# Longer weight runs, a reordered load queue and a new split of the casts in a batched matmul

## The chip, the cores and the metric

The kernel runs on one core of a Trainium2 chip. The metric is the device time of one execution in microseconds, the median of several runs. A profiled execution gives a trace; its span, from the first to the last instruction, is 1 to 2 us shorter than the timed figure. TensorE appears as PE (its weight loads as PEld), VectorE as DVE, ScalarE as ACT, GpSimd as POOL and SyncE, which issues all transfers, as SP.

## The reference

```python
b1, b2, m, k, n = 8, 16, 256, 512, 384
x:      (8, 16, 256, 512) float32
weight: (8, 16, 512, 384) float32
out = np.matmul(x, weight)          # 128 independent products
```

The inputs are 167.77 MB and the output 50.33 MB, so 218.1 MB have to cross between memory and the core.

## The kernel before

The 128 products are worked in 32 groups of G = 4. For each group the kernel loads weights and x as float32, casts both to bf16, transposes x on TensorE, copies the transposes out of PSUM, multiplies, copies the products out of PSUM and stores them.

```python
XS, WS, OS = 2, 2 * G // D, 4          # buffers: x, weight halves (D = 2), output
def load(e, t, U, s):                   # SyncE, group n
    for d in range(G // D):             # two transfers, 12 KB per partition each
        e.wait_ge(w_cast, ...)          # the slot's casts are done
        e.dma_start(w_sb[slot][:], w_rows[...].rearrange("(p k) n -> p k n", k=S * KO))
    e.wait_ge(x_cast, ...)
    e.dma_start(x_sb[s % XS][:], ...)   # 16 KB per partition

def prepare(e, t, U, s):                # VectorE
    ...                                 # 8 casts of 64 partitions x 1536 columns
    for q in range(T):                  # T = 4: transposes out of PSUM
        e.wait_ge(t_made, ...)
        e.tensor_copy(out=x_t[...], in_=pt[...].bitcast(bf16))

# ScalarE: 4 casts of x, then 4 copies of products out of PSUM
# SyncE, in its loop: load(n + 4); store(n)
```

TensorE does 16 transposes and 128 matmuls a group. A store of group n is issued after the loads of group n + 4; the copy of group n + 4 into its output buffer waits until that store has landed.

Of the kernel before, what the change touches and what calls it, by code (L numbers as in the profile page):

```python
# [12 lines left out]
def kernel(  # L13
# [6 lines left out]
    nc = tc.nc  # L20
    P = 128

    b1, b2, M, K = x.shape
    _, _, _, N = weight.shape
    B = b1 * b2
    KO = K // P

    x_rows = x.rearrange("b1 b2 m k -> (b1 b2 m) k")
    w_rows = weight.rearrange("b1 b2 k n -> (b1 b2 k) n")
# [3 lines left out]
    bf16 = mybir.dt.bfloat16  # L33
# [6 lines left out]
    G = 4  # L40
    C = P // G
    R = G * M // P
    T = R // 2
    D = 2
    S = 2
    HP = P // D
    NG = B // G

    XS, WS, OS = 2, 2 * G // D, 4
    BS, TS, WBS = 1, 2, 2 * G  # L50
    PT, PO = 4, 2

    LAG = 4

    ctx.enter_context(tc.tile_critical(no_gpsimd_drain=True))  # L55

    def sbuf(name, shape, dtype, n):
        return [
            ctx.enter_context(nc.sbuf_tensor(f"{name}{s}", shape, dtype)) for s in range(n)
        ]  # L60
# [6 lines left out]
    def sems(name, n):  # L67
        return [tc.alloc_semaphore(f"{name}{s}") for s in range(n)]
# [2 lines left out]
    identity = sbuf("identity", [P, P], fp32, 1)[0]  # L71
    x_sb = sbuf("x_sb", [P, R, K], fp32, XS)

    x_bf = sbuf("x_bf", [P, R, S, HP, KO], bf16, BS)
    x_t = sbuf("x_t", [P, R, KO // 2, P, 2], bf16, TS)
    w_sb = sbuf("w_sb", [P, S * KO, N], fp32, WS)
    w_bf = sbuf("w_bf", [P, KO, N], bf16, WBS)
# [4 lines left out]



    id_done, x_cast, w_cast, t_made, t_copied, p_made, o_copied = (
        sems(name, 1)[0]
        for name in (
            "id_done", "x_cast", "w_cast", "t_made", "t_copied", "p_made", "o_copied"
        )
    )  # L90
    x_in, w_in, o_out = sems("x_in", XS), sems("w_in", WS), sems("o_out", OS)


    BIAS = 8


    def load(e, t, U, s):
        n = t * U + s
        for d in range(G // D):
            slot = (s * (G // D) + d) % WS  # L100
            if not isinstance(n, int) or n >= 2:
                e.wait_ge(w_cast, n * (G * S) + ((d + 1) * D * S - 2 * G * S))
            e.dma_start(  # L103
                w_sb[slot][:],
                w_rows[bass.ds(n * (G * K) + d * (D * K), D * K)].rearrange(
                    "(p k) n -> p k n", k=S * KO
                ),
            ).then_inc(w_in[slot], 16)
        if not isinstance(n, int) or n >= XS:
            e.wait_ge(x_cast, n * T + (1 - XS) * T)  # L110
        e.dma_start(  # L111
            x_sb[s % XS][:],
            x_rows[bass.ds(n * (G * M), G * M)].rearrange("(p r) k -> p r k", r=R),
        ).then_inc(x_in[s % XS], 16)

    def store(e, t, U, s, pieces=1):
        n = t * U + s
        dram = o_rows[bass.ds(n * (G * M), G * M)].rearrange("(p r) n -> p r n", r=R)
        for q in range(pieces):
            rows = slice(q * R // pieces, (q + 1) * R // pieces)  # L120
            e.wait_ge(o_copied, n * T + ((q + 1) * T // pieces + BIAS))
            e.dma_start(out=dram[:, rows], in_=out_sb[s % OS][:, rows]).then_inc(
                o_out[s % OS], 16
            )

    def cast_x(e, t, U, s, q):
        n = t * U + s
        if q == 0:
            e.wait_ge(x_in[s % XS], (t * (U // XS) + s // XS) * 16 + 16)
        e.wait_ge(t_made, n * T + (q + 1 - T + BIAS))  # L130
        rows = slice(2 * q, 2 * q + 2)
        e.copy(  # L132
            out=x_bf[s % BS][:, rows],
            in_=x_sb[s % XS][:, rows].rearrange("p r (q s c) -> p r s q c", s=S, c=KO),
        ).then_inc(x_cast, 1)

    def prepare(e, t, U, s):
        n = t * U + s
        e.wait_ge(p_made, n * T + (BIAS - T))
        for d in range(G // D):  # L140
            slot = (s * (G // D) + d) % WS
            e.wait_ge(
                w_in[slot], (t * (U * G // D // WS) + s * G // D // WS) * 16 + 16
            )
            for a in range(D):
                for h in range(S):
                    e.tensor_copy(  # L147
                        out=w_bf[(s * G + d * D + a) % WBS][h * HP : (h + 1) * HP],
                        in_=w_sb[slot][a * HP : (a + 1) * HP, h * KO : (h + 1) * KO, :],
                    ).then_inc(w_cast, 1)  # L150
        for q in range(T):
            e.wait_ge(t_made, n * T + (q + 1 + BIAS))
            e.tensor_copy(  # L153
                out=x_t[s % TS][:, 2 * q : 2 * q + 2],
                in_=pt[(s * T + q) % PT][:].bitcast(bf16),
            ).then_inc(t_copied, 1)

    def multiply(e, t, U, s):
        n = t * U + s
        words = x_bf[s % BS][:].rearrange("p r s q c -> p r (s q c)").bitcast(fp32)  # L160
        for q in range(T):
            e.wait_ge(x_cast, n * T + (q + 1))
            e.wait_ge(t_copied, n * T + (q + 1 - PT + BIAS))
            for rr in range(2):
                for h in range(KO // 2):
                    ins = e.transpose(  # L166
                        pt[(s * T + q) % PT][:, rr, h, :],
                        words[:, 2 * q + rr, h :: KO // 2],
                        identity[:],
                    )  # L170
            ins.then_inc(t_made, 1)
        e.wait_ge(w_cast, n * (G * S) + G * S)
        for q in range(T):
            e.wait_ge(t_copied, n * T + (q + 1 + BIAS))
            e.wait_ge(o_copied, n * T + (q + 1 - PO + BIAS))
            for rr in range(2):
                for ko in range(KO):
                    for i in range(G):
                        mine = slice(i * C, (i + 1) * C)
                        ins = e.matmul(  # L180
                            po[(s * T + q) % PO][mine, rr, :N],
                            x_t[s % TS][:, 2 * q + rr, ko // 2, mine, ko % 2],
                            w_bf[(s * G + i) % WBS][:, ko, :],
                            start=(ko == 0),
                            stop=(ko == KO - 1),
                        )
            ins.then_inc(p_made, 1)

    def copy_out(e, t, U, s, q):
        n = t * U + s  # L190
        if q == 0:
            e.wait_ge(o_out[s % OS], (t * (U // OS) + s // OS) * 16 + 16)
        e.wait_ge(p_made, n * T + (q + 1 + BIAS))  # L193
        e.copy(  # L194
            out=out_sb[s % OS][:, 2 * q : 2 * q + 2, :],
            in_=po[(s * T + q) % PO][:, :, :N],
        ).then_inc(o_copied, 1)
# [7 lines left out]
    def on_sync(e):  # L205
        U = OS
        for n in range(LAG):
            load(e, 0, NG, n)
        rounds = (NG - LAG) // U
        with e.Fori(0, rounds) as t:  # L210
            for s in range(U):
                load(e, t, U, LAG + s)
                store(e, t, U, s)
        for n in range(rounds * U, NG):
            if n + LAG < NG:
                load(e, 0, NG, n + LAG)
            store(e, 0, NG, n, T if n == NG - 1 else 1)
        for s in range(OS):
            e.wait_ge(o_out[s], 16 + 16 * (NG // OS + (T - 1 if s == (NG - 1) % OS else 0)))

    def on_vector(e):
        U = 2
        e.sem_inc(t_copied, BIAS)
        with e.Fori(0, NG // U) as t:
            for s in range(U):
                prepare(e, t, U, s)

    def on_tensor(e):
        U = 2
        e.sem_inc(t_made, BIAS)  # L230
        e.sem_inc(p_made, BIAS)
        e.wait_ge(id_done, 2)

        pe = mybir.EngineType.PE
        with nc.Fori(0, NG // U, engines=OrderedEngineSet([pe]), head_slot={pe: 0}) as t:
            for s in range(U):
                multiply(e, t, U, s)

    def on_scalar(e):
        U = OS  # L240
        e.sem_inc(o_copied, BIAS)
        for s in range(OS):
            e.sem_inc(o_out[s], 16)

        with e.Fori(0, NG // U) as t:
            for s in range(U):
                for q in range(T):
                    cast_x(e, t, U, s, q)
                for q in range(T):
                    copy_out(e, t, U, s, q)  # L250

    on_gpsimd(nc.gpsimd)
    on_sync(nc.sync)
    on_vector(nc.vector)
    on_tensor(nc.tensor)
    on_scalar(nc.scalar)


# [28 lines left out]
```

## Time and profile before

| | before |
|---|---|
| time, median of 4 runs | 518.18 us (517.86 to 518.6) |
| span of the profiled execution | 517.2 us |
| busiest compute engine | VectorE, 64% |
| share of 16 DMA engines' time filled by packets | 99.3% |
| mean rate | 422 GB/s |

The lines behind this are shown and read in the prediction. The DMA share stays at 1 until 511 us, so the kernel is bound by its transfers. And what is left after the last landing (x of group 31, at 496.66 us) is short: casts of x, transposes, matmuls and copies are over at 507.72 us.

### The profile page before, as it was taken

Reading aid. Unit: us, or ns where it says so; the run is one execution under the profiler, and the core shown is the slowest. Engines: PE = TensorE matmul, PEld = TensorE weight load, DVE = VectorE, ACT = ScalarE, POOL = GpSimd, SP = SyncE. Lnnn points to the kernel's source line nnn. Section 1 sums busy time; section 2 is a strip of 40 time slices with the busy share of each in tenths; the row PEclk is TensorE's granted clock in tenths of the full one; section 3 lists DMA queues with packets and bytes.
Section 4 is the critical chain, followed back from the end, with each engine's and each line's share of the span. In section 5 each row is a group of like instructions: output and inputs, shape, how many; then the busy total and the mean of one; then the engine's idle time right before and its main releaser. Section 6 shows DMA issues by size and latency. Waiting matters only on the chain.

```text
span 517.2 us, 11523 instructions
## 1 busy us (share of the span) xinstructions
PE 306.6 (59%) x4608; PEld 200.6 (39%) x4608; DVE 332.8 (64%) x384; ACT 236.7 (46%) x264; POOL 0.7 (0%) x6
## 2 busy tenths in 40 slices
PE   0478776556665457645577554776446765467752
PEld 0345444334443334433344332444324443244431
DVE  3698875667556676556675566855658656676550
ACT  0465564443644436435355354454444544544441
POOL 0000000000000000000000000000000000000000
PEclk9998877878777887878777778877788877778777
DMA  8999999999999999999999999999999999999996
GB/s 340 430 423 424 424 432 426 429 428 430 432 427 427 427 428 432 429 427 430 426 431 431 426 429 430 427 432 427 427 429 429 427 433 425 430 428 430 429 428 251
DMA packets 18869, 218.18 MB, mean 422 GB/s; under 512 B 2096, under 2 KB 2096, under 8 KB 2608
## 3 DMA queue, kind: packets, MB, share of 16 engines
q1 hardware_dynamic: 18864, 218.11, 99.3%
q8 instruction: 3, 0.05, 0.0%
q14 instruction: 2, 0.02, 0.0%
HBM read 167.77 MB, written 50.33 MB: 422 GB/s over the span
## 4 chain that ended last, share of the span: by engine, by line
DMA 81%; ACT 10%; PE 4%; issue 3%; ACTq 0%; SPq 0%
DMA x_sb<-in_x_dram 81%; ACT x_bf L132 9%; PE po L180 2%; PE pt L166 1%; ACTq L130 0%; ACT out_sb L194 0%; SPq L111 0%; SPq L103 0%; ACT L132 0%; ACTq L193 0%; SPq L282 0%; SPq L55 0%
## 5 line engine op out<-in xcount | busy, mean ns | idle before, releaser
L147 DVE CAST w_bf<-w_sb 64x1536 bf16<-64x1536 f32 x256 | 244.4, 955 | 47.2 <-DMA w_sb<-in_weight_dram 38.5
L166 PE MATMUL pt<-identity,x_bf 128*128 128x128 f32 x512 | 123.7, 425 | 199.3 <-ACT x_bf L132 199.1
L180 PE MATMUL po<-w_bf,x_t 128*32 128x384 bf16 x4096 | 185.1, 342 | 1.0 <-issue 1.0
L166 PEld LDWEIGHTS pt<-identity,x_bf 128*128 128x128 f32 x512 | 91.8, 216 | 232.1 <-issue 218.3
L194 ACT COPY out_sb<-po 128x768 f32<-128x768 f32 x128 | 102.2, 798 | 147.2 <-PE po L180 147.2
L153 DVE COPY x_t<-pt 128x1024 bf16<-128x1024 bf16 x128 | 88.4, 691 | 122.3 <-PE pt L166 121.8
L132 ACT CAST x_bf<-x_sb 128x1024 bf16<-128x1024 f32 x128 | 124.4, 1042 | 80.9 <-DMA x_sb<-in_x_dram 80.8
L180 PEld LDWEIGHTS po<-w_bf,x_t 128*32 128x32 bf16 x4096 | 108.8, 101 | 73.8 <-issue 14.2
L132 ACT ACT_TABLE_LOAD x8 | 10.3, 1283 | 42.9 <-DMA x_sb<-in_x_dram 42.9
masks.py:199 POOL TENSOR_SCALAR_AFFINE_SELECT identity<-identity 128x128 f32<-128x128 f32 x1 | 0.3, 292 | 0.2 <-POOL identity L200 0.2
L200 POOL MEMSET identity<- 128x128 f32 x1 | 0.2, 204 | 0.5 <-SPq L55 0.5
L271 POOL MEMSET const-bfloat16-1.0<- 128x1 bf16 x1 | 0.1, 101 | 0.0
L271 POOL MEMSET const-uint8-127<- 128x1 uint8 x1 | 0.1, 101 | 0.0
L271 POOL MEMSET const-float32-0.0<- 128x1 f32 x1 | 0.1, 98 | 0.2 <-issue 0.2
L271 POOL MEMSET const-float32-1.0<- 128x1 f32 x1 | 0.1, 98 | 0.0
## 6 DMA issues: line engine op xcount, KB each, us to landing
w_sb<-in_weight_dram SPq DMA_DIRECT2D x64, 1536.0 KB, 27.5
x_sb<-in_x_dram SPq DMA_DIRECT2D x32, 2048.0 KB, 27.5
out_dram<-out_sb SPq DMA_DIRECT2D x31, 1536.0 KB, 30.7
out_dram<-out_sb SPq DMA_DIRECT2D x4, 384.0 KB, 5.9
```

Of the source, the lines that this page charges most:

```text
L132: e.copy(out=x_bf[s % BS][:, rows], in_=x_sb[s % XS][:, rows].rearrange("p r (q s c) -> p r s q c", s=S, c=KO),).then_inc(x_cast, 1)
L147: e.tensor_copy(out=w_bf[(s * G + d * D + a) % WBS][h * HP : (h + 1) * HP], in_=w_sb[slot][a * HP : (a + 1) * HP, h * KO : (h + 1) * KO, : ...
L153: e.tensor_copy(out=x_t[s % TS][:, 2 * q : 2 * q + 2], in_=pt[(s * T + q) % PT][:].bitcast(bf16),).then_inc(t_copied, 1)
L166: ins = e.transpose(pt[(s * T + q) % PT][:, rr, h, :], words[:, 2 * q + rr, h :: KO // 2], identity[:],)
L180: ins = e.matmul(po[(s * T + q) % PO][mine, rr, :N], x_t[s % TS][:, 2 * q + rr, ko // 2, mine, ko % 2], w_bf[(s * G + i) % WBS][:, ko, :], ...
L194: e.copy(out=out_sb[s % OS][:, 2 * q : 2 * q + 2, :], in_=po[(s * T + q) % PO][:, :, :N],).then_inc(o_copied, 1)
L200: e.memset(identity[:], 0.0).then_inc(id_done, 1)
L271: nc = _bacc.Bacc("TRN2", target_bir_lowering=False, num_devices=1)
```

## The change

The intent is fewer and longer transfers: one weight load a group with 24 KB runs in place of two with 12 KB. With 16 consecutive rows of one product on a partition, a product's weights then lie on 32 partitions, so a group needs 16 casts of 32 partitions where it had 8 of 64. To pay for them the work is dealt anew: VectorE casts x and 12 of the 16 weight pieces, ScalarE casts 4 pieces and empties PSUM both times. The queue's order becomes x, store, weights; the loads of the last two groups go ahead of the stores that are left.

```diff
-    D = 2
-    S = 2
-    XS, WS, OS = 2, 2 * G // D, 4
+    S = P // C
+    XS, WS, OS = 2, 2, 4
+    LAG, LATE = 4, 2
+    CA, CL = 4, 1
+    CV = G * S - CA
@@ load_w
-            e.dma_start(w_sb[slot][:], w_rows[... d * (D * K), D * K)] ...)   # twice
+            w_sb[s % WS][:],
+            w_rows[bass.ds(n * (G * K), G * K)].rearrange("(p k) n -> p k n", k=S * KO),
@@ SyncE
-                load(e, t, U, LAG + s)
-                store(e, t, U, s)
+                load_x(e, t, U, LAG + s)
+                store(e, t, U, s)
+                load_w(e, t, U, LAG + s)
 ...
+        for n in range(NG - LATE, NG):
+            load_x(e, 0, NG, n)
+            load_w(e, 0, NG, n)
+        for n in range(NG - LATE - LAG, NG):
             store(...)
@@ VectorE
-                prepare(e, t, U, s)
+            for q in range(T):
+                cast_x(e, t, U, s, q)
+            cast_w(e, t, U, s, range(parts))
@@ ScalarE, one step
+            copy_out(e, t, U, s, 0)
+            copy_out(e, t, U, s, 1)
+            cast_w(e, t, U, s + 1, parts[:1])
+            copy_out(e, t, U, s, 2)
+            cast_w(e, t, U, s + 1, parts[1:2], False)
+            copy_out(e, t, U, s, 3)
+            cast_w(e, t, U, s + 1, parts[2:], False)
+            evacuate(e, t, U, s + 1)
```

The diff is cut: semaphores, counts and the unrolled ends are left out. In the last group VectorE casts 11 pieces and ScalarE 5.

More of the change, by code (lines that the diff above doesn't have):

```diff
@@ L43 @@
     T = R // 2
-    D = 2
-    S = 2
-    HP = P // D
+    S = P // C
     NG = B // G
-    XS, WS, OS = 2, 2 * G // D, 4
+    XS, WS, OS = 2, 2, 4
     BS, TS, WBS = 1, 2, 2 * G
     PT, PO = 4, 2
-    LAG = 4
+    LAG, LATE = 4, 2
+    CA, CL = 4, 1
+    CV = G * S - CA
     ctx.enter_context(tc.tile_critical(no_gpsimd_drain=True))
@@ L72 @@
     x_sb = sbuf("x_sb", [P, R, K], fp32, XS)
-    x_bf = sbuf("x_bf", [P, R, S, HP, KO], bf16, BS)
+    x_bf = sbuf("x_bf", [P, R, S, C, KO], bf16, BS)
     x_t = sbuf("x_t", [P, R, KO // 2, P, 2], bf16, TS)
@@ L80 @@
     po = psum("po", [P, 2, 512], fp32, PO)
-    id_done, x_cast, w_cast, t_made, t_copied, p_made, o_copied = (
+    id_done, x_cast, w_vcast, w_acast, t_made, t_copied, p_made, o_copied = (
         sems(name, 1)[0]
         for name in (
-            "id_done", "x_cast", "w_cast", "t_made", "t_copied", "p_made", "o_copied"
+            "id_done", "x_cast", "w_vcast", "w_acast",
+            "t_made", "t_copied", "p_made", "o_copied",
         )
@@ L94, with load_x @@
     BIAS = 8
-    def load(e, t, U, s):
+    def load_x(e, t, U, s):
         n = t * U + s
-        for d in range(G // D):
-            slot = (s * (G // D) + d) % WS
-            if not isinstance(n, int) or n >= 2:
-                e.wait_ge(w_cast, n * (G * S) + ((d + 1) * D * S - 2 * G * S))
-            e.dma_start(
-                w_sb[slot][:],
-                w_rows[bass.ds(n * (G * K) + d * (D * K), D * K)].rearrange(
-                    "(p k) n -> p k n", k=S * KO
-                ),
-            ).then_inc(w_in[slot], 16)
         if not isinstance(n, int) or n >= XS:
@@ L114, in load, with load_w @@
         ).then_inc(x_in[s % XS], 16)
+    def load_w(e, t, U, s):
+        n = t * U + s
+        if not isinstance(n, int) or n >= WS:
+            e.wait_ge(w_vcast, n * CV + (1 - WS) * CV)
+            e.wait_ge(w_acast, n * CA + (1 - WS) * CA)
+        e.dma_start(
+            w_sb[s % WS][:],
+            w_rows[bass.ds(n * (G * K), G * K)].rearrange("(p k) n -> p k n", k=S * KO),
+        ).then_inc(w_in[s % WS], 16)
     def store(e, t, U, s, pieces=1):
@@ L131, in cast_x @@
         rows = slice(2 * q, 2 * q + 2)
-        e.copy(
+        e.tensor_copy(
             out=x_bf[s % BS][:, rows],
@@ L135, in cast_x, with cast_w, evacuate @@
         ).then_inc(x_cast, 1)
-    def prepare(e, t, U, s):
+    def cast_w(e, t, U, s, parts, first=True):
+        n = t * U + s
+        if first:
+            e.wait_ge(p_made, n * T + (BIAS - T))
+            e.wait_ge(w_in[s % WS], (t * (U // WS) + s // WS) * 16 + 16)
+        copy = e.tensor_copy if e is nc.vector else e.copy
+        for c in parts:
+            i, h = c // S, c % S
+            copy(
+                out=w_bf[(s * G + i) % WBS][h * C : (h + 1) * C],
+                in_=w_sb[s % WS][i * C : (i + 1) * C, h * KO : (h + 1) * KO, :],
+            ).then_inc(w_vcast if c < CV else w_acast, 1)
+    def evacuate(e, t, U, s):
         n = t * U + s
         e.wait_ge(p_made, n * T + (BIAS - T))
-        for d in range(G // D):
-            slot = (s * (G // D) + d) % WS
-            e.wait_ge(
-                w_in[slot], (t * (U * G // D // WS) + s * G // D // WS) * 16 + 16
-            )
-            for a in range(D):
-                for h in range(S):
-                    e.tensor_copy(
-                        out=w_bf[(s * G + d * D + a) % WBS][h * HP : (h + 1) * HP],
-                        in_=w_sb[slot][a * HP : (a + 1) * HP, h * KO : (h + 1) * KO, :],
-                    ).then_inc(w_cast, 1)
         for q in range(T):
             e.wait_ge(t_made, n * T + (q + 1 + BIAS))
-            e.tensor_copy(
+            e.copy(
                 out=x_t[s % TS][:, 2 * q : 2 * q + 2],
@@ L171, in multiply @@
             ins.then_inc(t_made, 1)
-        e.wait_ge(w_cast, n * (G * S) + G * S)
+        e.wait_ge(w_acast, n * CA + CA)
+        e.wait_ge(w_vcast, n * CV + CV)
         for q in range(T):
@@ L207, in on_sync @@
         for n in range(LAG):
-            load(e, 0, NG, n)
-        rounds = (NG - LAG) // U
+            load_x(e, 0, NG, n)
+            load_w(e, 0, NG, n)
+        rounds = (NG - LATE - LAG) // U
         with e.Fori(0, rounds) as t:
             for s in range(U):
-                load(e, t, U, LAG + s)
+                load_x(e, t, U, LAG + s)
                 store(e, t, U, s)
-        for n in range(rounds * U, NG):
-            if n + LAG < NG:
-                load(e, 0, NG, n + LAG)
+                load_w(e, t, U, LAG + s)
+        for n in range(LAG + rounds * U, NG - LATE):
+            load_x(e, 0, NG, n)
+            store(e, 0, NG, n - LAG)
+            load_w(e, 0, NG, n)
+        for n in range(NG - LATE, NG):
+            load_x(e, 0, NG, n)
+            load_w(e, 0, NG, n)
+        for n in range(NG - LATE - LAG, NG):
             store(e, 0, NG, n, T if n == NG - 1 else 1)
@@ L222, in on_vector, with step @@
         U = 2
-        e.sem_inc(t_copied, BIAS)
-        with e.Fori(0, NG // U) as t:
+        def step(t, U, s, parts):
+            for q in range(T):
+                cast_x(e, t, U, s, q)
+            cast_w(e, t, U, s, range(parts))
+        with e.Fori(0, NG // U - 1) as t:
             for s in range(U):
-                prepare(e, t, U, s)
+                step(t, U, s, CV)
+        step(0, NG, NG - 2, CV)
+        step(0, NG, NG - 1, CV - CL)
     def on_tensor(e):
@@ L240, in on_scalar @@
         U = OS
+        e.sem_inc(t_copied, BIAS)
         e.sem_inc(o_copied, BIAS)
@@ L243, in on_scalar, with step @@
             e.sem_inc(o_out[s], 16)
-        with e.Fori(0, NG // U) as t:
-            for s in range(U):
-                for q in range(T):
-                    cast_x(e, t, U, s, q)
-                for q in range(T):
-                    copy_out(e, t, U, s, q)
+        def step(t, U, s, more=0):
+            parts = list(range(CV - more, CV + CA))
+            copy_out(e, t, U, s, 0)
[6 more added lines that the diff above has]
+            evacuate(e, t, U, s + 1)
+        evacuate(e, 0, NG, 0)
+        cast_w(e, 0, NG, 0, range(CV, CV + CA))
+        rounds = (NG - 2) // U
+        with e.Fori(0, rounds) as t:
+            for s in range(U):
+                step(t, U, s)
+        for n in range(rounds * U, NG - 1):
+            step(0, NG, n, CL if n == NG - 2 else 0)
+        for q in range(T):
+            copy_out(e, 0, NG, NG - 1, q)
     on_gpsimd(nc.gpsimd)
```

## The prediction

> **What bounds the kernel now.** I read the summary first, to see which engine is never idle.
>
> ```profile
> PE 306.6 (59%) x4608; PEld 200.6 (39%) x4608; DVE 332.8 (64%) x384; ACT 236.7 (46%) x264; POOL 0.7 (0%) x6
> ...
> DMA  8999999999999999999999999999999999999996
> ...
> q1 hardware_dynamic: 18864, 218.11, 99.3%
> ...
> DMA 81%; ACT 10%; PE 4%; issue 3%; ACTq 0%; SPq 0%
> ```
>
> No compute engine passes 64%; the DMA row is full in every slice but the ends, the queue's packets fill 99.3% of 16 engines' span, and the chain that ended last is 81% DMA. Then I cut the span into stretches (columns: busy time of PE, PEld, DVE, ACT and POOL with counts, granted clock, DMA share, GB/s).
>
> ```profile
> 4.00:46.00 42.00, 20.17 (x300) 13.67 (x300) 29.68 (x34) 19.23 (x21) 0.00 (x0) 0.97 1.01 428
> ...
> 238.00:302.00 64.00, 40.41 (x576) 25.68 (x576) 42.02 (x49) 29.60 (x33) 0.00 (x0) 0.76 1.01 429
> ...
> 494.00:506.00 12.00, 8.17 (x128) 5.94 (x132) 4.68 (x6) 5.86 (x7) 0.00 (x0) 0.72 1.01 427
> ...
> 511.00:512.00 1.00, 0.00 (x0) 0.00 (x0) 0.00 (x0) 0.00 (x0) 0.00 (x0) 0.70 0.67 270
> 512.00:513.00 1.00, 0.00 (x0) 0.00 (x0) 0.00 (x0) 0.00 (x0) 0.00 (x0) 0.50 0.28 111
> 513.00:514.00 1.00, 0.00 (x0) 0.00 (x0) 0.00 (x0) 0.00 (x0) 0.00 (x0) 0.50 0.16 65
> ```
>
> Loads alone (to 46 us), loads with stores (the middle) and stores alone (after the last load landed at 496.66) all run at 427 to 429 GB/s with a share of 1. So 218.11 MB take 218.11/428.5 = 509.0 us. The stretch to 4 us moved 0.50 MB, as if the queue had started at full rate at 2.8 us; 2.8 + 509.0 = 511.8. The span is 517.2: the other 5.4 us are the end, where the 16 engines finish unevenly (share 0.67, 0.28, 0.16) and the last completions come in. There is almost no starvation to remove. A group moves 6.816 MB (3.146 weights, 2.097 x, 1.573 out), or 15.9 us.
>
> The costs of the instructions that move come from the groups and the opening of the timeline:
>
> ```profile
> L147 DVE CAST w_bf<-w_sb 64x1536 bf16<-64x1536 f32 x256 | 244.4, 955 | 47.2 <-DMA w_sb<-in_weight_dram 38.5
> ...
> L194 ACT COPY out_sb<-po 128x768 f32<-128x768 f32 x128 | 102.2, 798 | 147.2 <-PE po L180 147.2
> ...
> L132 ACT CAST x_bf<-x_sb 128x1024 bf16<-128x1024 f32 x128 | 124.4, 1042 | 80.9 <-DMA x_sb<-in_x_dram 80.8
> ...
> L132 ACT ACT_TABLE_LOAD x8 | 10.3, 1283 | 42.9 <-DMA x_sb<-in_x_dram 42.9
> ```
>
> (page, groups: line, engine, operation, tiles, count, busy us, mean ns, idle before)
>
> ```profile
> 8.71 7.86 DVE L147 CAST w_bf<-w_sb 64x1536 bf16<-64x1536 f32 x8 [8.71 <-DMA w_sb<-in_weight_dram]
> ...
> 17.37 1.28 ACT L132 ACT_TABLE_LOAD   x1 [17.37 <-DMA x_sb<-in_x_dram]
> 18.67 3.89 ACT L132 CAST x_bf<-x_sb 128x1024 bf16<-128x1024 f32 x4
> ```
>
> [...]
>
> **The change, part by part.**
>
> Transfers. The bytes stay. 64 weight loads of 12 KB runs become 32 of 24 KB: 4096 fewer weight packets and 32 x 16 = 512 fewer small completion packets, 4608 of 18,864. [...]
>
> VectorE. It cast 8 halves and emptied 4 transposes a group. Now it casts 12 quarter-lane pieces of the same 1536 columns: [...] each is 955 ns at the measured pitch of 7.86/8 = 0.983: 11.8 us. The x casts have 1024 columns[...]. Sum **14.7 us a group** against 15.9 of DMA: VectorE goes to some 92% and stays below the transfer[...].
>
> ScalarE. It loses 3.9 us of x casts and the table load in its loop (the order of instructions has it once now, ahead of the loop, not every fourth group). It gains 4 weight casts[...]; and 4 evacuations of 1024 columns[...]. With 3.2 us of out copies: **12.9 us**, some 13.5 with gaps. Also below 15.9.
>
> Steady waits. Let w(n) land at L. ScalarE's pieces are done by about L + 7, its evacuations by L + 11.5, VectorE's by L + 11.8; only then do the matmuls of n run and w(n+2) go out. Queued ahead of it at L are x(n+1), a store and w(n+1), 15.9 us of transfer, then x(n+2), whose slot came free with the casts of x(n) just before L, and a store, another 8.6. So w(n+2) is wanted 24.5 us after L and issued at 11.8: the queue keeps 10 us or more in hand. That is less than now (a load lands 27.5 us after its issue), but it does not run dry.
>
> Start. x now comes before the weights: x(0) lands at 2.8 + 4.9 + 2.25 = 10 us (2.25 is landing beyond data, from x(0) of before: 5.24 MB end at 15.1, landed at 17.4), w(0) at 17.3. VectorE: w(0) 17.3 to 29.1, x(1) to 32.0, w(1) to 43.8. The queue's first four loads end at 27.3, x(2) at 32.2, w(2), issued 29.1, at 39.5, x(3) at 44.4, and w(3), issued at 43.8 with 1.85 to start (as the first DMA), begins at 45.7: about **+1.2 us** empty, once. Afterwards stores stretch the DMA period to 15.9 and VectorE catches up 1.2 us a group.
>
> End. Six stores, not four, wait behind the last load. After w(31) lands, 11 VectorE casts take 10.8 us, the matmuls 5.4, the last copy 0.8: the last piece of store 31 goes out 17.0 us after, when stores 26 to 30 (18.4 us) are just ending. The queue does not starve, nor did it before, so the change gains **0** there; the uneven finish stays.
>
> Sum: 517.2 - 1.0 + 1.2 + 0 = 517.4 us of span; the timed median lies 1.2 above the span: about 518.5. As the start may hide in uneven engines, I say 518.0.
>
> **The rivals.**
> (a) VectorE becomes the bound. [...] For it: [...] no strided VectorE cast in the trace. [...] Chance 8%.
> (b) The larger run frees the queue [...]. Against: loads of 16 KB and 12 KB runs show one rate. [...]
> (c) The shallower queue (10 us at its lowest, where 16 engines end 4 us apart) lets fast engines run dry each group: 0.2 us a group would be +6 us, 1.2%. For it: VectorE at 92% has 1.2 us to spare a group.
>
> **Range and chances.** The middle case holds by bytes that no part of the change touches[...]. (b) and (c) stretch it to 513.5 and 522. Faster by over 2% needs a span below 507[...]: 2%. Slower by over 2% is (a) or a strong (c): 9%.
>
> **What would show it.** Right: DMA share still 1.00 and 427 to 431 GB/s in the middle; some 14,250 packets; [...] weight casts at 955, VectorE busy near 460 us; [...] one table load; a dip in DMA share at 40 to 47 us; the finish still uneven. Wrong: [...] VectorE without idle time and DMA share under 0.95 (rival a); [...] a DMA share of 0.97 to 0.99 in every group (c).

Passages are cut from the prediction, each marked. The sums still hold terms that are cut: VectorE's 14.7 us a group one for the casts of x beside the 11.8 us of weight casts, ScalarE's 12.9 us (and L + 7 and L + 11.5, which rest on it) those for the weight casts and the evacuations beside the 3.2 us of output copies, and the 517.4 us of span a -1.0 for the longer transfers, whose derivation is cut. Without that term the sum is 518.4. The range, 513.5 to 522, stands.

## The result and the profile after

The changed kernel took 526.2 us (525.54 to 526.4, 4 runs) against 518.18. The ratio is 1.0152, 95% interval 1.0134 to 1.017. All ratios here divide the mean time of one kernel's fast runs by that of the other's in the same rounds, so they are not quite the ratio of the medians. 526.2 lies above the predicted range, which ended at 522.

The page of the changed kernel, in the rows shown of before (busy time by engine, DMA share in 40 slices, the queue, the chain that ended last):

```profile
PE 305.7 (58%) x4608; PEld 205.6 (39%) x4608; DVE 443.6 (85%) x511; ACT 406.6 (78%) x386; POOL 0.7 (0%) x6
...
DMA  8999999999999999999999999999999999999993
...
q1 hardware_dynamic: 14256, 218.11, 98.1%
...
DMA 54%; DVE 28%; issue 13%; PE 2%; ACT 2%; DVEq 1%; SPq 0%
```

The bytes are the same and the packets are as foretold. The last slice fell from 6 to 3 tenths, and VectorE now holds 28% of the chain that ended last. The groups (line, engine, operation, tiles, count, busy us, mean ns, idle before):

```profile
L149 DVE CAST w_bf<-w_sb 32x1536 bf16<-32x1536 f32 x383 | 364.1, 951 | 55.3 <-DMA w_sb<-in_weight_dram 44.3
...
L149 ACT CAST w_bf<-w_sb 32x1536 bf16<-32x1536 f32 x129 | 189.4, 1468 | 2.6 <-DMA w_sb<-in_weight_dram 0.2
...
L159 ACT COPY x_t<-pt 128x1024 bf16<-128x1024 bf16 x128 | 120.3, 1027 | 0.8
L136 DVE CAST x_bf<-x_sb 128x1024 bf16<-128x1024 f32 x128 | 80.0, 689 | 11.0 <-DMA x_sb<-in_x_dram 10.0
```

A weight cast on VectorE took 951 ns with 32 partitions, where it had taken 955 with 64 (ScalarE took 1.47 us for either in e10). Over the 32 groups VectorE was busy 13.9 us a group and ScalarE 12.7, against 14.7 and 12.9 in the forecast, so the error was not in what these cost. The stretches of the trace show where the time went (us, busy time of PE, PEld, DVE, ACT, POOL, granted clock, DMA share, GB/s):

```profile
36.00:48.00 12.00, 6.88 (x104) 4.92 (x100) 11.69 (x15) 10.70 (x11) 0.00 (x0) 0.86 1.00 408
48.00:60.00 12.00, 6.52 (x104) 4.59 (x96) 11.69 (x15) 11.40 (x11) 0.00 (x0) 0.85 0.98 366
54.00:56.00 2.00, 0.00 (x0) 0.00 (x0) 1.94 (x3) 1.95 (x3) 0.00 (x0) 1.00 1.11 352
56.00:58.00 2.00, 0.27 (x4) 0.17 (x8) 1.94 (x3) 2.00 (x3) 0.00 (x0) 0.60 0.98 225
...
238.00:302.00 64.00, 37.88 (x580) 25.54 (x578) 56.36 (x66) 51.76 (x50) 0.00 (x0) 0.81 1.01 431
...
478.00:484.00 6.00, 1.27 (x20) 0.76 (x24) 5.84 (x8) 4.80 (x5) 0.00 (x0) 0.64 0.87 337
490.00:496.00 6.00, 2.04 (x16) 1.85 (x16) 5.81 (x7) 5.88 (x6) 0.00 (x0) 1.00 0.85 309
510.00:516.00 6.00, 3.84 (x52) 1.96 (x56) 0.00 (x0) 5.62 (x6) 0.00 (x0) 0.53 0.23 98
```

The middle runs at 431 GB/s, a little faster than the 429 of before. There are holes in three places: at 36 to 60 us, at 478 to 496 us, and at 510 to 516 us, where the queue is all but empty. They are not of one kind. At 510 to 516 us the DMA share falls with the rate (0.23 at 98 GB/s), from 478 to 496 us it falls less than the rate does (0.92 at 349 GB/s, where a share of 1 went with 431). At 54 to 58 us, the deepest part of the first hole, the share stays at 1.11 and 0.98 while the rate falls to 352 and 225 GB/s: the DMA engines were busy, but their packets took longer (those of x, 16 KB each, 0.88 us at the median against 0.61 in the middle). Against 429 GB/s these 4 us lose 1.3 us, more than half of what the start loses. The end in order of time (start, length, engine, line, operation):

```profile
482.49 0.33 SPq L115 DMA_DIRECT2D w_sb<-in_weight_dram  x1
...
484.91 11.75 DVE L149 CAST w_bf<-w_sb 32x1536 bf16<-32x1536 f32 x12
...
499.10 10.76 DVE L149 CAST w_bf<-w_sb 32x1536 bf16<-32x1536 f32 x11
500.22 0.80 ACT L201 COPY out_sb<-po 128x768 f32<-128x768 f32 x1 [0.90 <-DMA out_dram<-out_sb]
...
506.62 4.45 ACT L149 CAST w_bf<-w_sb 32x1536 bf16<-32x1536 f32 x3
511.09 3.76 ACT L159 COPY x_t<-pt 128x1024 bf16<-128x1024 bf16 x4
512.16 7.84 PE L187 MATMUL po<-w_bf,x_t 128*32 128x384 bf16 x128 [6.09 <-ACT x_t L159]
...
520.05 0.80 ACT L201 COPY out_sb<-po 128x768 f32<-128x768 f32 x1 [0.50 <-PE po L187]
```

The last weights (group 31) are issued at 482.49, when VectorE is done with group 29 and a slot is free; the trace has the last of their 16 arrivals at 496.3. VectorE is busy with group 30 and x until 499.1. ScalarE ends its casts of group 31 at 511.07 and only then empties the transposes, for which the matmuls wait. The last copy is over at 520.85, 24.5 us after the landing. In the kernel before it was 11.1 us after.

### The profile page after: what moved, and what is told of

Same layout as the page of the kernel before. It is cut to its first block, busy times and chain, and to the rows that moved or that the text cites. A ratio compares the mean times of both kernels' runs of the same rounds, so it can differ in the third digit from the quotient of the medians.

```text
span 524.6 us, 11607 instructions
## 1 busy us (share of the span) xinstructions
PE 305.7 (58%) x4608; PEld 205.6 (39%) x4608; DVE 443.6 (85%) x511; ACT 406.6 (78%) x386; POOL 0.7 (0%) x6
## 4 chain that ended last, share of the span: by engine, by line
DMA 54%; DVE 28%; issue 13%; PE 2%; ACT 2%; DVEq 1%; SPq 0%
DMA w_sb<-in_weight_dram 54%; DVE w_bf L149 26%; PE po L187 2%; DVE x_bf L136 1%; ACT w_bf L149 1%; ACT out_sb L201 0%; DVEq L243 0%; ACT x_t L159 0%; SPq L115 0%; DVEq L134 0%; SPq L105 0%; DVEq L145 0%; SPq L321 0%; SPq L58 0%
## 5 line engine op out<-in xcount | busy, mean ns | idle before, releaser
L149 DVE CAST w_bf<-w_sb 32x1536 bf16<-32x1536 f32 x383 | 364.1, 951 | 55.3 <-DMA w_sb<-in_weight_dram 44.3
L187 PE MATMUL po<-w_bf,x_t 128*32 128x384 bf16 x4096 | 236.4, 405 | 203.5 <-DVE w_bf L149 170.0
L187 PEld LDWEIGHTS po<-w_bf,x_t 128*32 128x32 bf16 x4096 | 140.5, 118 | 293.3 <-ACT x_t L159 193.9
L149 ACT CAST w_bf<-w_sb 32x1536 bf16<-32x1536 f32 x129 | 189.4, 1468 | 2.6 <-DMA w_sb<-in_weight_dram 0.2
L159 ACT COPY x_t<-pt 128x1024 bf16<-128x1024 bf16 x128 | 120.3, 1027 | 0.8
L136 DVE CAST x_bf<-x_sb 128x1024 bf16<-128x1024 f32 x128 | 80.0, 689 | 11.0 <-DMA x_sb<-in_x_dram 10.0
L172 PE MATMUL pt<-identity,x_bf 128*128 128x128 f32 x512 | 71.4, 293 | 10.8 <-DVE x_bf L136 10.8
L172 PEld LDWEIGHTS pt<-identity,x_bf 128*128 128x128 f32 x512 | 65.1, 209 | 20.7 <-issue 20.7
```

Source lines behind the costliest of these rows:

```text
L136: e.tensor_copy(out=x_bf[s % BS][:, rows], in_=x_sb[s % XS][:, rows].rearrange("p r (q s c) -> p r s q c", s=S, c=KO),).then_inc(x_cast, 1)
L149: copy(out=w_bf[(s * G + i) % WBS][h * C : (h + 1) * C], in_=w_sb[s % WS][i * C : (i + 1) * C, h * KO : (h + 1) * KO, :],).then_inc(w_vcas ...
L159: e.copy(out=x_t[s % TS][:, 2 * q : 2 * q + 2], in_=pt[(s * T + q) % PT][:].bitcast(bf16),).then_inc(t_copied, 1)
L172: ins = e.transpose(pt[(s * T + q) % PT][:, rr, h, :], words[:, 2 * q + rr, h :: KO // 2], identity[:],)
L187: ins = e.matmul(po[(s * T + q) % PO][mine, rr, :N], x_t[s % TS][:, 2 * q + rr, ko // 2, mine, ko % 2], w_bf[(s * G + i) % WBS][:, ko, :], ...
```

## The experiments

My first theory (A) was that the end costs the time: loads without stores between them come faster than VectorE takes them. The rival (B) was the start and a slower pace throughout. All runs below are of 4 to 6 timed executions, with the kernel before in the same rounds.

### e1_late0: stores interleaved to the end

```diff
-    LAG, LATE = 4, 2
+    LAG, LATE = 4, 0
```

> The changed kernel with its stores interleaved with the loads to the very end (no last two groups loaded ahead of the held-back stores). Theory A, the end costs: in the changed kernel the last loads come without stores between, so faster (12.2 us of transfer a group) than VectorE can take them (14.2 us), the queue runs dry at 478 to 496 us, and the last group's casts start late because VectorE is still at the group before. Then this run loses the dip in the DMA rate before the last load lands, VectorE starts on the last weights within 1 us of their landing, and the time falls by 3 to 6 us, to 520 to 523 (ratio to the kernel before 1.004 to 1.010). Rival B, the loss lies in the start (queue dry at 38 to 60 us) and in a slower pace of the whole: then it stays at 525 to 527 (1.014 to 1.017).

Measured: 527.19 us, ratio 1.0167 (1.0153 to 1.018). This is a miss. The hole at 478 to 496 us did go (419 to 449 GB/s there), and VectorE took the last weights at once. But with two more stores ahead of them, those weights landed at 501.3, not 496.3. From there to the last copy it took 20.8 us in place of 24.5, so the chain won 3.7 us and the landing lost 5.0: the span ended at 526.3, 1.7 us later. So the holes before the last landing are not the main cost; how long the chain after it is, and how many stores lie behind it to hide it, is.

### e2_before_late2: the kernel before, with two groups loaded ahead

```diff
+        for n in range(NG - LATE, NG):
+            load(e, 0, NG, n)
+        for n in range(NG - LATE - LAG, NG):
+            store(...)
```

> The kernel before with its last two groups loaded ahead of the stores, as the changed kernel does. If holding the stores back is harmful in itself (rival: reads without writes, or a burst of stores at the end, move slower), it loses 3 to 5 us here too (1.006 to 1.010). Under theory A the harm needs a VectorE slower than the loads alone; here VectorE needs 10.6 us a group against 12.2, so the time stays within 1.5 us (0.997 to 1.003) and the queue has no dip before the last load.

Measured: 519.82 us, ratio 1.0023 (1.0009 to 1.0037). Both forecasts for theory A held: under 1.5 us, and no dip before the last load (424 to 430 GB/s from 478 to 502 us). So holding stores back costs 1.2 us here, little but clear of noise, without any longer casts. The reading of theory A, that the harm needs them, was too strong: e9 and e12 below find 2.4 and 1.4 us where the casts at the end are short. The trace also held the mechanism, which I saw only in e7:

```profile
496.46 1.50 ACT L194 COPY out_sb<-po 128x768 f32<-128x768 f32 x2 [12.01 <-DMA out_dram<-out_sb]
```

ScalarE stood idle for 12.0 us before its copies of group 30 for store 26 (landed at 496.4), and the last copy ended at 514.6, not 507.7.

### e3_split12: 12 KB runs in the changed kernel

```diff
+        for d in range(2):
+            half = slice(d * S * KO // 2, (d + 1) * S * KO // 2)
+            e.dma_start(w_sb[s % WS][:, half], rows[:, half]).then_inc(w_in[s % WS], 16)
```

> The changed kernel with each group's weights loaded in two transfers whose runs are 12 KB, as before, in place of one with 24 KB; nothing else. If fewer, longer packets are what raised the rate in the middle of the kernel from 428.5 to 431 GB/s, the middle returns to 428 to 429, the groups to a pitch of 15.9 us, and the time rises by 2 to 3 us, to 528 to 529 (1.019 to 1.021). If the rate came from the order of the transfers, it stays at 431 and the time at 526 (1.014 to 1.017).

Measured: 527.03 us, ratio 1.016 (1.0146 to 1.0174). The middle (238 to 302 us) of this run:

```profile
238.00:302.00 64.00, 38.13 (x583) 26.02 (x581) 55.92 (x66) 51.50 (x51) 0.00 (x0) 0.81 1.01 429
```

The rate is back at 429, so the run length is what raised it. Yet the time rose by less than 1 us, not by 2 to 3, and the ratio by 0.0008 (0.4 us), which is within the noise. Between 152.8 us and the landing of the weights 18 groups later, the pitch was 15.95 us here and 15.85 in the changed kernel: 0.1 us a group, 1.6 us over these 18. In the end VectorE was still busy with group 30 when the last weights landed at 497.3, 1.0 us later than in the changed kernel, and the last copy ended 0.6 us later.

### e4_wx_late0: weights before x

The order of loads and of VectorE's casts is turned round. ScalarE's first casts, of group 0, also move ahead of its first evacuation.

```diff
-    LAG, LATE = 4, 2
+    LAG, LATE = 4, 0
@@ SyncE, loop (first and last groups alike)
-                load_x(e, t, U, LAG + s)
-                store(e, t, U, s)
-                load_w(e, t, U, LAG + s)
+                load_w(e, t, U, LAG + s)
+                store(e, t, U, s)
+                load_x(e, t, U, LAG + s)
@@ VectorE, one step
+            cast_w(e, t, U, s, range(parts))
             for q in range(T):
                 cast_x(e, t, U, s, q)
-            cast_w(e, t, U, s, range(parts))
```

> The changed kernel with weights before x in the queue and in VectorE's program, and the stores interleaved to the end. What follows the last landing is then the 2.5 us of x casts, transposes and matmuls (some 11 us in the kernel before), not 10.8 us of weight casts and then the matmuls (25 us in the changed kernel). Theory A extended: the end returns to that of the kernel before, the start improves as weights 0 are cast while x 0 lands, and the middle keeps its 431 GB/s: 515 to 518 (0.994 to 1.000). If the loss lay in the split of work over the engines and not in the order, it stays at 522 or more.

Measured: 528.19 us, ratio 1.0187 (1.0164 to 1.0209). Another miss. The x of the last group lands 8.8 us after its weights (508.8 against 500.1), but the 11 casts of these take 10.8 us, so x waits and is cast after them: the last copy ends 22 us after VectorE began on the weights (500.17 to 522.3). And the holes of the start grew (410 GB/s from 46 to 110 us). Order alone does not shorten the chain. The time itself is less clear: the five runs spread from 526.75 to 529.76, and in this trace the last of the 16 arrivals of a load comes 7.3 us after the 15th at the end (1.4 in the changed kernel), which puts off both landings. What makes it trail was not tested.

### Cutting the casts: e5_endcut, e6_startcut, e7_bothcut

Three kernels with a wrong result measure what the casts cost at the ends. The transfers stay; chosen groups cast 16 of 384 columns.

```diff
-                out=w_bf[(s * G + i) % WBS][h * C : (h + 1) * C],
+                out=w_bf[(s * G + i) % WBS][h * C : (h + 1) * C, :, :cols(n)],
+    CUT = (30, 31)             # e5; e6: (0, 1, 2, 3); e7: (0, 1, 2, 3, 30, 31)
+    def cols(n):
+        return 16 if isinstance(n, int) and n in CUT else N
+        for b in w_bf:                       # GpSimd, at the start, in e6 and e7
+            e.memset(b[:], 0.0).then_inc(w_zero, 1)
```

In e6 and e7 the first four groups are also taken out of the loops, and the first casts wait for the clearing on GpSimd.

> Wrong result on purpose: the changed kernel with the weight casts of the last two groups (30 and 31) cut to 16 of their 384 columns, on VectorE and ScalarE alike, so that each costs some 0.2 us in place of 0.95 and 1.47; all transfers, waits and instruction counts stay. Theory A2, the end is set by the work that is left after the last landing (12 us of casts and evacuations, 8 of matmuls, 4 of copy and store, measured from 499 us), not by the transfers: the time falls by 6 to 9 us, to 517 to 520 (ratio to the kernel before 0.998 to 1.004), and the DMA rate has no hole at 478 to 496 and at 510 to 520 us. Rival, the end is set by the held-back stores and their waits: it falls by less than 3 us.

> Wrong result on purpose: the same cut in the first four groups (0 to 3) only, with a clearing of the cast buffers on the idle GpSimd ahead of them. Theory: the holes in the DMA rate at 38 to 60 us come from VectorE's 14.2 us a group against 12.2 of loads with two slots; without them the stretch from 46 to 110 us goes from 417 to 430 GB/s, every later event comes 2 to 3 us earlier, and the time falls by as much, to 523 to 524.5 (1.009 to 1.012). If the start is hidden by the end's chain of casts, nothing changes: 526 (1.015).

> Wrong result on purpose: both cuts, first four and last two groups. If start and end are the whole loss and they add, what is left is the kernel before with the faster middle (431 against 428.7 GB/s, 3 us): 514.5 to 517 (0.993 to 0.998). If it stays above 519, a third cause is missing.

Measured: e5 522.19 us (1.008, 1.0065 to 1.0095), e6 524.42 (1.012, 1.0105 to 1.0135), e7 520.48 (1.0042, 1.0029 to 1.0055). From 1.0152, the end's casts are worth 0.0072 (3.7 us), the start's 0.0032 (1.7 us) and both together 0.011 (5.7 us), so within the noise they add. The narrowed casts took 0.21 us each on VectorE in e7 (12 in 2.56 us) and 0.24 to 0.26 on ScalarE. The time of e6 came out as expected. The end was worth less, and against the expectation the hole at 478 to 496 us stayed in e5 (361 GB/s), so it does not come from the casts of the last two groups. And e7 stayed above 519: a third cause was missing. Its timeline points to one:

```profile
493.75 2.35 DVE L154 CAST w_bf<-w_sb 32x64 bf16<-32x64 f32 x11 [3.55 <-DMA w_sb<-in_weight_dram]
497.40 1.50 ACT L206 COPY out_sb<-po 128x768 f32<-128x768 f32 x2 [5.32 <-DMA out_dram<-out_sb]
```

ScalarE stood idle for 5.3 us ahead of its copy of group 30, for the store of group 26, whose buffer it needs (there are four). LATE = 2 puts that store behind the last weights. ScalarE's work on group 31 stands behind this copy in its program.

### e8_ca5: one more cast on ScalarE

```diff
-    CA, CL = 4, 1
+    CA, CL = 5, 0
```

> A correct kernel: 5 of the 16 weight casts on ScalarE in place of 4 in every group (11 on VectorE; the last group's extra one on ScalarE is then gone, so its split stays 11 to 5). VectorE's pace falls from 14.2 to 13.3 us a group, ScalarE's rises from some 12.7 to 14.1, both under the 15.8 of the transfers. Theory: less queueing behind VectorE at the start (1 us a group for three groups) and before the last group (1 to 2 us), 522 to 524.5 (1.007 to 1.012). Rival: ScalarE, which ends the chain of casts and evacuations, becomes the late one, and the time stays or rises: 526 or more.

Measured: 533.22 us, ratio 1.0289 (1.0275 to 1.0302), slower than the changed kernel by 7 us. The time is the rival's. The waits of this run (engine line waited for: us in total, times, longest):

```profile
PE po L187 <- ACT x_t L159: 183.1, 30, 6.2
```

ScalarE empties the transposes after its casts, and in 30 groups the matmuls wait for it (in 6 in the changed kernel). In the middle the transfers hide that (431 GB/s from 238 to 302 us); at 466 to 472 and 484 to 490 us the rate was 326 and 179. The last weights landed at 501.3, 5.0 us later than in the changed kernel, and from there to the last copy it took 27.8 us in place of 24.5. For the later landing there is a rival that I did not test: here too the last arrival trails the 15th, by 5.7 us at 475 us (1.8 in the changed kernel). How much of the 5.0 us is ScalarE's and how much is that of the trailing DMA engine stays open.

### e9_bothcut_late0: both cuts, no held-back stores

```diff
-    LAG, LATE = 4, 2                         # as in e7
+    LAG, LATE = 4, 0
```

> Wrong result on purpose: both cuts as before (casts of groups 0 to 3, 30 and 31 narrowed), and the stores interleaved to the end instead of two of them held back. With both cuts ScalarE still waited 5.3 us at 492 us for store 26, which the holding back puts behind the last loads: with four output buffers the copy of group 30 needs it. Theory: this is the third cause, and without it the end is the transfers' alone: 514.5 to 517 (ratio to the kernel before 0.993 to 0.998). If it stays at 519 or more, a cause is still missing.

Measured: 518.6 us, ratio 0.9996 (0.9982 to 1.001); wrong like e7. Against e7 it gains 0.0046 (2.4 us), but it misses the 514.5 to 517 that I expected. The three causes give 0.0156 (8.1 us): the loss is accounted for, the gain of the longer runs is not there. The 2.4 us stand for all that holding back does: besides the wait for store 26, the rate at 478 to 496 us is 421 GB/s here and 370 in e7. With the casts (e1), undoing it gained nothing, as the later landing cost more than the shorter chain won.

### Correct kernels that mend it: e10_mixed, e11_mixed_tail, e12_mixed_late2

Groups at the ends go back to two 12 KB transfers and 8 casts of 64 partitions, 6 on VectorE and 2 on ScalarE; the rest keeps 24 KB runs.

```diff
+    HEAD, TAIL = 4, 2                       # e11: 0, 2
+    HALF = [*range(HEAD), *range(NG - TAIL, NG)]
-    LAG, LATE = 4, 2
+    LAG, LATE = 4, 1                        # e12: 4, 2
+            for c in parts:                 # half-lane groups
+                i, h = c // 2, c % 2
+                copy(out=w_bf[...][h * 64 : (h + 1) * 64],
+                     in_=w_sb[s % WS][a * 64 : (a + 1) * 64, ...])
```

> A correct kernel meant to beat both: 24 KB runs and quarter-lane casts for groups 4 to 29 only. Groups 0 to 3, 30 and 31 get their weights in two transfers of 12 KB runs and in 8 half-lane casts, 6 on VectorE and 2 on ScalarE, so a group costs VectorE 8.4 us, not 14.2; one group is loaded ahead of the held-back stores, not two. If start, end and held-back stores are the whole loss, it keeps the gain of the longer runs (1 to 3 us) and loses nothing: 515 to 517.5 (0.993 to 0.998). If the new split of work costs something else, it stays above 519.

> The same with half-lane groups at the end only (30 and 31); the start as in the changed kernel. The start's holes cost 2 us here: 517 to 519.5 (0.997 to 1.002), 2 above the run with both.

> The kernel with half-lane groups at start and end, but two groups loaded ahead of the held-back stores, as in the changed kernel. If holding two back stalls the copies of group 30 behind store 26, it is 2 to 4 us slower than with one: 517.5 to 520.5. If the stall is hidden, both are equal within 1 us.

| | time, us | ratio to before | 95% |
|---|---|---|---|
| e10, start and end mended, one held back | 518.75 | 1.0001 | 0.9987 to 1.0015 |
| e11, end mended only | 520.85 | 1.0042 | 1.0028 to 1.0055 |
| e12, as e10, two held back | 520.19 | 1.0027 | 1.0013 to 1.0041 |

These confirm the causes in kernels with correct results: e10 wins back the whole 8 us, the start is worth 2.1 us of it (e11 less e10), and the second held-back group 1.4 us (e12 less e10). But e10 only equals the kernel before; I had expected 515 to 517.5, and e11 missed its range in the same way. The gain of the longer runs was missing.

### e13_mixed_end: a shorter chain in the last group

```diff
+            copy_out(e, 0, NG, NG - 2, q)        # all of group 30 first
+        evacuate(e, 0, NG, NG - 1)               # no casts of group 31 on ScalarE
```

VectorE casts all 8 halves of group 31 instead; the rest is as in e10.

> The correct kernel with half-lane groups at start and end and one group loaded ahead of the stores, with one thing changed in its end: ScalarE copies out all of group 30 first and casts no weights of group 31; VectorE casts all 8 halves of it. In the run it comes from, ScalarE's copies 2 and 3 of group 30 stood behind a cast that waited for the last weights (1.6 us), and the last copy ended at 509.3 us, 1.6 later than in the kernel before, although 0.64 MB (1.5 us) more had been moved by 504. If that chain eats the gain of the longer runs, the last copy ends by 507.5 us and the time falls by 1 to 2.5 us, to 516.3 to 517.7 (0.995 to 0.998). If the longer runs gain nothing that reaches the end, it stays at 518.5 (0.999 to 1.001).

Measured: 518.63 us, ratio 1.0 (0.9986 to 1.0013). The chain did get shorter: the last copy ended at 506.76, 1.0 us before that of the kernel before. It made no difference. The same stretches of e13 and of the kernel before show why; first e13:

```profile
510.00:511.00 1.00, 0.00 (x0) 0.00 (x0) 0.00 (x0) 0.00 (x0) 0.00 (x0) 0.50 0.43 172
...
512.00:513.00 1.00, 0.00 (x0) 0.00 (x0) 0.00 (x0) 0.00 (x0) 0.00 (x0) 0.50 0.06 25
...
514.00:515.00 1.00, 0.00 (x0) 0.00 (x0) 0.00 (x0) 0.00 (x0) 0.00 (x0) 0.50 0.05 22
```

And before:

```profile
510.00:511.00 1.00, 0.00 (x0) 0.00 (x0) 0.00 (x0) 0.00 (x0) 0.00 (x0) 1.00 1.02 412
...
514.00:515.00 1.00, 0.00 (x0) 0.00 (x0) 0.00 (x0) 0.00 (x0) 0.00 (x0) 0.50 0.07 28
```

A share of 0.06 is one engine of 16 (1/16 = 0.0625). In e13 most engines are done by 512, and a single one works until 515. The trace also has each transfer's 16 arrivals. For the store of group 30:

| arrivals of store 30, us | 8th | 15th | 16th |
|---|---|---|---|
| before | 508.3 | 510.4 | 512.1 |
| e13 | 506.8 | 508.5 | 511.6 |

In e13 most engines are 1.5 to 1.9 us ahead, and the last one 0.4. The kernel waits for all 16 arrivals of a transfer, so the gain does not reach the end: the last store is complete at 515.3 in e13 and at 515.8 before. That the last engine is slower, and not just later, the same arrivals show: from store 27 to store 29 the 15th comes every 3.6 us and the 16th every 4.0, in both kernels. Why it is slower, and whether it is the same engine in every run, the runs do not show.

## Why the prediction was wrong

**Transfers.** I said -1 us, an estimate for which no trace gave the ground. The sign was right. The mean gained more, some 2 us by an estimate (431 against 429 GB/s over the whole; e3 takes it back), but the engine that finishes last gained 0.4 us (e13).

**VectorE, ScalarE and the steady waits.** These were right in the main: 14.2 us a group on VectorE against 14.7 said, and in the middle a DMA share of 1.01. Rivals (a), VectorE as the bound everywhere, and (c), engines running dry in every group, did not come; nor did (b), a queue freed by the longer runs, as the middle ran at 431 GB/s against 429. One term was off: for ScalarE's weight casts I counted on an overlap such as the casts of x show in the kernel before (four took 3.89 us at 1.042 each), but four of them took 5.94 us at 1.468 each, with no overlap.

**Start.** I said +1.2 us at 40 to 47 us. The holes are at 36 to 60 us and worth about 2 us (e6, e11): more than one group is affected, as loads alone need 12.2 us a group (an estimate: 5.24 MB at 429 GB/s) and VectorE 14.2 (2.50 and 11.75 in the timeline). And the wait that I foretold, an empty queue, is the smaller part: at 54 to 58 us the engines were busy with slow packets. The same stretch ran at 289 GB/s in the changed kernel, at 384 with the casts narrowed (e6) and at 418 with half-lane casts (e10), so the casts have a part in it, by themselves or through the order in which the transfers then come; why the packets slow down is not shown.

**End.** This is the step that failed: "the last piece of store 31 goes out 17.0 us after, when stores 26 to 30 (18.4 us) are just ending ... so the change gains **0** there". Four things were wrong in it.

1. I let VectorE begin when w(31) lands. It began 2.8 us later, since the loads of groups 30 and 31, with no stores between, come in faster than VectorE casts them.
2. I counted VectorE's 10.8 us of casts and left out ScalarE, which has four copies of group 30, five casts and the evacuations in program order. I had its evacuations done 11.5 us after a landing; here the last one ended 18.5 us after (514.85). The matmuls began 13.1 us after VectorE's start (499.10 to 512.16), not 10.8.
3. I took 5.4 us for the matmuls, as in the kernel before, where the granted clock was 1.00 from 501.5 to 506.9 us; they took 7.9. TensorE had been idle since 506.1 us, the granted clock fell to 0.50 at 510.4 us, 4.3 us later, and it stayed at 0.50 until 517.2 us, through some 5 us of matmuls. I did not reckon with this.
4. I overlooked that the held-back store 26 keeps ScalarE from copying group 30, with four output buffers. ScalarE waited 0.9 us for it in the changed kernel, 5.3 in e7 and 12.0 in e2; holding back a second group cost 1.4 us of the time in e12.

Together these make 24.5 us from landing to the last copy in place of 17.0 (the wait of point 4 lies within point 2), which the five stores behind the landing no longer cover: hence the almost empty queue at 510 to 516 us. The shares measured are 3.7 us for the casts at the end, 1.7 to 2.1 for the start, and 2.4 for the held-back stores once the casts are out of the way; their sum, 8.1 us, is the loss. That e1, undoing only the held-back stores, won nothing shows that these shares depend on the order in which they are removed.

I also read the uneven finish of the kernel before (0.67, 0.28, 0.16, ...) as a tail that stays, and did not see in it that the last engine sets the end (a share of 0.07, one engine, from 514 to 515 us), so that a better mean rate need not help.

## What to carry to other kernels

Where transfers bound the middle, work out the end separately: list everything that each engine has in program order after the last landing, at the clock it will then have (here 0.50 from 512 to 517 us), and compare it with the transfers left behind that landing. Casting twice as many pieces for a longer run cost nothing in the middle, where the transfer hid it (431 GB/s against 429), and was paid at start and end, so use the cheaper form in the first and last groups. And read a DMA share of about 1/16 at the end (0.05 to 0.07 from 512 to 515 us in e13) as one engine: here that one set the end, and a better mean rate gained nothing.
